# Input-projection weight tiles split by a casting load, a negated copy and an accumulating load

## The chip, the cores and the metric

The kernel runs on 1 core of one Trainium2 chip. The metric is device time of one execution in microseconds. Engines: TensorE (PE), VectorE (DVE), ScalarE (ACT), GpSimd (POOL) and SyncE (SP). SP and POOL issue DMAs, which run on the core's 16 DMA engines; the profile shows SP's transfers on the hardware queue q1 and POOL's on the software queue q0.

## What is computed

One inference step of a decoder layer (width 1024) for 512 prompt tokens and 8 sample tokens, 520 columns together. One input projection `w_in` of 8 x 1024 columns feeds a chunkwise recurrence (HGRN2, 8 heads of 128), a second recurrence (RG-LRU, 8 blocks of 128) and two merge gates; then come branch projections, an output projection and an MLP.

```python
h = _rmsnorm(x, norm1_g[l]) * (1.0 + sc1) + sh1
u = h @ w_in[l].astype(F32)
qa, fa, ia, oga, xb, yb, ga, gb = _split_cols(u)
...
merged = (jax.nn.sigmoid(ga) * (o_a @ w_branch_a[l].astype(F32))
          + jax.nn.sigmoid(gb) * (o_b @ w_branch_b[l].astype(F32)))
x = (x.astype(F32) + g1 * (merged @ w_out[l].astype(F32))).astype(dt)
h2 = _rmsnorm(x, norm2_g[l]) * (1.0 + sc2) + sh2
ff = jnp.square(jax.nn.relu(h2 @ w_ff1[l].astype(F32))) @ w_ff2[l].astype(F32)
x = (x.astype(F32) + g2 * ff).astype(dt)
```

## The kernel before

To keep float32 accuracy, the kernel splits each operand into a high part in the type float32r and the remainder, a low part in the same type, and adds three products: high by high, high by low, low by high (`products`, L148). The activations `h` are split once; the weights come in tiles of 1024 x 128 (in SBUF 128 x 8 x 128, 512 KB), and each tile is split when it arrives. A tile is used by `gemm` (L160): 8 steps of k, 3 products, 2 halves of the 520 columns, that is 48 matmuls of 260 columns into one PSUM pair `mm` (two such pairs rotate), 32 of them with the high part and 16 with the low one.

`weights` lists the tiles of the whole program up to the MLP in the order of use. The input projection has 56 whole tiles here: the first three are split by hand in `begin`, 53 pass through `ready_w` (L134), called by `take_w` as each tile is taken. It starts loads up to `LOADS` = 3 ahead of the split, and splits each tile `AHEAD` = 2 tiles before its use. A load (`_load_w`, L103) is issued by SP into `wst`, a pool of `WST` = 4 staging buffers of 512 KB. A split (`_split_w`, L107) is a cast on ScalarE to `whi` (L113) and a subtraction on VectorE to `wlo` (L116), both in the pool `whl`, with two pairs of buffers at this stage (`split_place` takes them in turn). Half of the last gate's columns are not whole tiles: they are loaded by POOL as `gw` (L866) and split in forms of their own.

The code is written as a list of steps (heads, recurrences, gates and so on); a scheduler decides the order of the instructions on each engine, which are then executed in that order. In `begin` the order on PE, ACT and DVE is the written one. POOL has little to do in the stage of the input projection: in the start the samples' columns (`fs`, `fsh`), and one root a head (`ss`, L231 and L232), which lies between ACT's sums of squares and ACT's scaling of that head's output. Later, in the MLP, POOL issues accumulating DMAs from SBUF to SBUF (`ma<-snap`, L1317 and L1335).

In the DMA issues, `wm<-in_w_piece` and `xT` are the first pieces that the program loads; the modulation of the input and the first products wait for them.

Of the kernel before, what the change touches and what calls it, by code (L numbers as in the profile page):

```python
# [6 lines left out]
F32 = mybir.dt.float32  # L7
F32R = mybir.dt.float32r
I32 = mybir.dt.int32
U8 = mybir.dt.uint8  # L10
AF = mybir.ActivationFunctionType
OP = mybir.AluOpType
# [8 lines left out]
KO = D // 128  # L21
# [9 lines left out]
NWM = 8  # L31
WST = 4
LOADS = 3
MODK = 7
FIRSTS = 3
ROWS = "rows"
MARK = "mark"
# [42 lines left out]
class Kernel:  # L80
# [7 lines left out]
    def weights(self, specs):  # L88


        self.wspecs, order, n = specs, [], 0
        for i, key in enumerate(specs):
            order.append((n - 1, 0, i) if ROWS in key else (n - AHEAD, 1, i))
            n += ROWS not in key
        self.worder = [(t, i) for t, _, i in sorted(order)]
        self.wstage, self.wsplit = {}, {}
        self.wnext_load = self.wnext_split = self.wcur = self.wtile = 0
        self.sw, self.nsplit, self.places = None, 0, []

    def _load_w(self, key, pool):  # L100
        src, r0, c0 = key[:3]
        st = pool.tile([128, KO, 128], F32, name="wst")
        self.nc.sync.dma_start(st.rearrange("p k n -> p (k n)"),  # L103
                               self.i[src][c0 // D - 2, r0 // 128] if ROWS in key else self.i[src][c0 // 128])
        return st

    def _split_w(self, st, place, after=None):  # L107
        if place is None:
            hi, lo = (self.wst.tile([128, KO, 128], F32R, tag="wst", name=n) for n in ("whi", "wlo"))
        else:  # L110
            pool = self.sw if place % 2 else self.whl
            hi, lo = (pool.tile([128, KO, 128], F32R, tag=f"{n}{place}", name=n, bufs=1) for n in ("whi", "wlo"))
        ins = self.nc.scalar.copy(hi, st)  # L113
        if after or self.start_act:
            self.behind(ins, after or self.start_act)
        self.nc.vector.tensor_tensor(lo, st, hi.bitcast(F32), OP.subtract)  # L116
        return hi, lo
# [15 lines left out]

    def ready_w(self, tile, loads=LOADS):  # L134
        while self.wnext_split < len(self.worder) and self.worder[self.wnext_split][0] <= tile:
            while self.wnext_load < min(self.wnext_split + loads, len(self.worder)):
                i = self.worder[self.wnext_load][1]
                self.wstage[i] = None if MARK in self.wspecs[i] else self._load_w(self.wspecs[i], self.wst)
                self.wnext_load += 1
            i = self.worder[self.wnext_split][1]  # L140
            st = self.wstage.pop(i)
            if ROWS in self.wspecs[i]:
                self.wsplit[i] = st.rearrange("p k n -> p (k n)")
            else:
                self.wsplit[i] = None if st is None else self._split_w(st, self.split_place())
            self.wnext_split += 1
# [13 lines left out]
    def gemm(self, keys, acts, extra=0, ps=None, after=None):  # L160

        ps = ps or self.pmm.tile([128, 2, 512], F32, name="mm")
        for q, key in enumerate(keys):
            hi, lo = self.take_w(key)
            for k in range(KO):
                n = q * KO + k
                self.products(ps, (hi[:, k], lo[:, k]), acts[n], n == 0, n == len(keys) * KO - 1, extra,
                              after=after)
                if self.mod_open and k == MODK:
                    self.mod_cols(*self.mod_open, after=self.last_product)  # L170
# [1904 lines left out]
```

## Time and profile before

| | |
|---|---|
| median of 3 runs (range) | 1007.01 us (1004.93 to 1007.44) |
| profiled execution | 1007.33 us, span 1005.5 us |
| busy PE, DVE, ACT, POOL | 985.9, 689.7, 524.4, 136.7 us |
| DMA hardware queue q1 | 123.47 MB, 36.3% of 16 engines |
| DMA software queue q0 | 18.70 MB, 8.5% of 16 engines |
| loads of `w_in` tiles (SP) | 56 of 512 KB, 3.6 us to landing |

Busy time of an engine is the time in which it executes at least one instruction. Matmuls are pipelined, so a group's mean duration is longer than the distance from one to the next. "Idle before" names what ended an engine's wait ahead of a group; the DMA rows give packets, MB and the share of 16 engines' time in the stretch that is asked for.

### The profile page before, as it was taken

The page shows a single profiled execution, that of the slowest core. Times are in us where ns is not written, and L with a number is a line of the kernel's source. Part 1 is how long each engine was busy: PE and PEld are TensorE (multiplying, and loading weights), DVE is VectorE, ACT ScalarE, POOL GpSimd, SP SyncE. Part 2 cuts the span into 40 slices and gives each one's busy share as a digit, 9 for nine tenths or more (in the row PEclk, how much of TensorE's full clock was granted, in tenths as well). Part 3 has the DMA queues.
Part 4 walks back from the last instruction along what each step waited for, and adds up shares of the span by engine and source line. Part 5 has one row for each costly group of instructions (what it writes and reads, how often), then busy time and mean ns, then how long its engine had stood idle before and what let it go on. Part 6 is the DMA issues. An engine that isn't in the chain of part 4 may idle for free. (4 is left out here: it accounts for less than half of the span.)

```text
span 1005.5 us, 23181 instructions
## 1 busy us (share of the span) xinstructions
PE 985.9 (98%) x9636; PEld 956.4 (95%) x9636; DVE 689.7 (69%) x1357; ACT 524.4 (52%) x997; POOL 136.7 (14%) x247
## 2 busy tenths in 40 slices
PE   7999999999999999989999999999999999999997
PEld 6899999999989999989999999999999999999996
DVE  6795966676595667886535456767767776768685
ACT  5565645734653572474412233466456645646662
POOL 1310000000000101121000000022321331232050
PEclk8999999999999999999999999999999999999999
DMA  9563343244234236345547665222752472272142
GB/s 348 216 209 128 102 159 124 81 145 132 98 133 153 100 99 212 111 148 179 185 168 270 241 212 199 84 85 53 177 151 81 104 192 85 65 183 70 64 85 86
DMA packets 48857, 143.67 MB, mean 143 GB/s; under 512 B 6240, under 2 KB 15904, under 8 KB 47720
## 3 DMA queue, kind: packets, MB, share of 16 engines
q1 hardware_dynamic: 37280, 123.47, 36.3%
q0 software_dynamic: 11456, 18.70, 8.5%
q8 instruction: 75, 1.23, 0.5%
q14 instruction: 30, 0.25, 0.1%
q10 hardware_dynamic: 16, 0.03, 0.0%
HBM read 123.65 MB, written 11.26 MB: 134 GB/s over the span
## 5 line engine op out<-in xcount | busy, mean ns | idle before, releaser
L155 PE MATMUL mm<-h,whi 128*128 128x260 f32 (+1 forms) x2720 | 451.6, 285 | 0.0
L155 PEld LDWEIGHTS mm<-h,whi 128*128 128x128 f32 x2720 | 378.5, 189 | 1.3 <-issue 0.6
L155 PE MATMUL mm<-h,wlo 128*128 128x260 f32 x1360 | 280.3, 286 | 2.6 <-DVE wlo L116 2.6
L116 DVE TENSOR_TENSOR wlo<-wst,whi 128x1024 fp32r<-128x1024 f32 x156 | 190.6, 1223 | 123.7 <-ACT whi L113 119.4
L113 ACT CAST whi<-wst 128x1024 fp32r<-128x1024 f32 x156 | 163.5, 1050 | 187.9 <-PE mm L155 147.3
L155 PEld LDWEIGHTS mm<-h,wlo 128*128 128x128 f32 x1360 | 212.4, 189 | 4.0 <-DVE wlo L116 3.2
L1293 POOL TENSOR_TENSOR ft<-ft,fsh 128x8 f32<-128x8 f32 x28 | 18.4, 658 | 209.1 <-DVE ft L1287 209.1
L1301 DVE TENSOR_TENSOR f<-f 128x260 f32<-128x260 f32 x64 | 27.3, 427 | 27.8 <-ACT f L1296 27.1
L1290 ACT ACTIVATE ft<-ft,fsh 128x512 f32<-128x512 f32 (+2 forms) x36 | 24.1, 676 | 36.1 <-DVE ft L1287 36.1
L155 PE MATMUL mm<-b,whi 128*128 128x260 f32 x256 | 41.6, 284 | 0.0
L155 PE MATMUL mm<-oa,whi 128*128 128x260 f32 x256 | 41.6, 285 | 0.0
L155 PE MATMUL mm<-a,whi 128*128 128x260 f32 x256 | 41.4, 284 | 0.0
L582 DVE TENSOR_TENSOR X<-X,tb 128x512 f32<-128x512 f32 x48 | 31.0, 688 | 12.6 <-PE ps L574 9.3
L155 PEld LDWEIGHTS mm<-oa,whi 128*128 128x128 f32 x256 | 34.9, 188 | 2.1 <-ACT whi L113 1.6
L155 PEld LDWEIGHTS mm<-b,whi 128*128 128x128 f32 x256 | 35.1, 189 | 1.7 <-ACT whi L113 1.2
L155 PEld LDWEIGHTS mm<-a,whi 128*128 128x128 f32 x256 | 35.0, 188 | 1.2 <-PE pt L359 0.8
L231 POOL TENSOR_SCALAR ss<-ss 128x4 f32<-128x4 f32 x8 | 2.7, 332 | 238.2 <-ACT g L666 238.1
L1335 POOL DMA_DIRECT2D ma<-snap x28 | 27.3, 989 | 37.5 <-issue 27.5
L179 ACT ACTIVATE gate<-pb,pa 128x260 f32<-128x260 f32 x32 | 15.4, 482 | 31.2 <-PE pb L714 31.2
L1317 POOL DMA_DIRECT2D ma<-snap x28 | 25.9, 926 | 41.0 <-DMA ma<-snap 25.6
L1296 ACT ACTIVATE f<-ft 128x520 f32<-128x520 f32 (+1 forms) x36 | 20.8, 587 | 15.0 <-POOL ft L1294 13.0
L155 PE MATMUL mm<-a,wlo 128*128 128x260 f32 x128 | 25.8, 283 | 0.0
(565 smaller groups left out, 2075.2 us busy)
## 6 DMA issues: line engine op xcount, KB each, us to landing
wst<-in_w_ff_dram SPq DMA_DIRECT2D x64, 512.0 KB, 3.7
wst<-in_w_in_dram SPq DMA_DIRECT2D x56, 512.0 KB, 3.6
wst<-in_w_mod_dram SPq DMA_DIRECT2D x32, 512.0 KB, 4.8
wm<-in_w_piece_dram SPq DMA_DIRECT2D x4, 1024.0 KB
wm<-in_w_rows_dram SPq DMA_DIRECT2D x4, 1024.0 KB, 11.4
st<-in_state_hgrn_dram SPq DMA_DIRECT2D x8, 512.0 KB, 3.9
vb<-vd SPq DMA_DIRECT2D x8, 512.0 KB, 3.9
out_dram<-st SPq DMA_DIRECT2D x8, 512.0 KB
```

The lines of the kernel that those rows point to most:

```text
L113: ins = self.nc.scalar.copy(hi, st)
L116: self.nc.vector.tensor_tensor(lo, st, hi.bitcast(F32), OP.subtract)
L155: self.last_product = self.nc.tensor.matmul(ps[s][:, :c.stop - c.start], x, y[:, c], start=first and n == 0, stop=last and n == 2)
L179: ins = self.nc.scalar.activation(out, x, AF.Sigmoid, **kw)
L231: p.tensor_scalar(out, x, n * EPS, None, OP.add)
L582: last = nc.vector.tensor_tensor(half, half, factors(tbs, x, b), OP.mult)
L1290: nc.scalar.activation(t[:, :p], t[:, :p], AF.Relu, bias=sh[:, 0:1])
L1293: eng.tensor_tensor(t[:, p:], t[:, p:], sh[:, 1:9], OP.add)
L1296: nc.scalar.activation(f, self.two(self.ft)[:, a:a + n], AF.Square)
L1301: self.nc.vector.tensor_tensor(f[:, n], f[:, a], f[:, b], op)
L1317: nc.gpsimd.dma_start(x[1][:, b], v[:, :n], accum_op=OP.add)
L1335: nc.gpsimd.dma_start(x[t][:, a], s[p], accum_op=OP.add)
```

## The change

The 53 tiles of `w_in` that pass through `ready_w` are split in another way. POOL issues a load that casts the tile from HBM into the float32r buffer of the high part (`_cast_w`, L117 in the changed file); ScalarE writes the negated high part into the low part's buffer (`_rest_w`, L122); POOL issues a second load of the same tile from HBM that adds it to that buffer (L125). Odd tiles take a pair of `whl`, even ones two of the four `wst` buffers, so four tiles have buffers at once. The cast of the next tile is issued in the code before the rest of the present one (`CASTS` = 2). All other tiles keep the former way.

```diff
+CASTS = 2
...
+    def _cast_w(self, key):
+        src = self.i[key[0]][key[2] // 128]
+        self.ncast += 1
+        if self.ncast % 2:
+            place = self.split_place()
+            hi, lo = (self.whl.tile([128, KO, 128], F32R, tag=f"{n}{place}", name=n, bufs=1) for n in ("whi", "wlo"))
+        else:
+            hi, lo = (self.wst.tile([128, KO, 128], F32, name="wst").bitcast(F32R) for _ in range(2))
+        self.nc.gpsimd.dma_start(hi.rearrange("p k n -> p (k n)"), src)
+        return hi, lo, src
+
+    def _rest_w(self, hi, lo, src):
+        ins = self.nc.scalar.activation(lo, hi.bitcast(F32), AF.Copy, scale=-1.0)
+        if self.start_act:
+            self.behind(ins, self.start_act)
+        self.nc.gpsimd.dma_start(lo.rearrange("p k n -> p (k n)"), src, accum_op=OP.add)
+        return hi, lo
...
     def ready_w(self, tile, loads=LOADS):
         while self.wnext_split < len(self.worder) and self.worder[self.wnext_split][0] <= tile:
-            while self.wnext_load < min(self.wnext_split + loads, len(self.worder)):
+            cast = self.wspecs[self.worder[self.wnext_split][1]][0] == "w_in"
+            while self.wnext_load < min(self.wnext_split + (CASTS if cast else loads), len(self.worder)):
                 i = self.worder[self.wnext_load][1]
-                self.wstage[i] = None if MARK in self.wspecs[i] else self._load_w(self.wspecs[i], self.wst)
+                key = self.wspecs[i]
+                self.wstage[i] = None if MARK in key else self._cast_w(key) if key[0] == "w_in" else self._load_w(key, self.wst)
...
-            if ROWS in self.wspecs[i]:
+            if self.wspecs[i][0] == "w_in":
+                self.wsplit[i] = self._rest_w(*st)
+            elif ROWS in self.wspecs[i]:
```

The scheduler places the new instructions. In the listings a row is a line of the code, the instruction, and what it writes from what; the names are the program's tiles with a buffer number.

POOL at the program's start, first before and then after the change:

```order
L237 IOTA jp_160 128x128
L247 MEMSET halfc_170 128x1
L72 TENSOR_TENSOR fs_123<-xsr_122,modT_108 128x16
L72 CAST h_157<-fs_123 128x2x8
L72 TENSOR_TENSOR h_158<-fs_123,h_157 128x2x8
```

```order
L262 IOTA jp_160 128x128
L272 MEMSET halfc_170 128x1
L117 DMA whi_471<-in_w_in_dram 128x1024
L117 DMA whi_670<-in_w_in_dram 128x1024
L117 DMA wst_474<-in_w_in_dram 128x1024
L73 TENSOR_TENSOR fs_123<-xsr_122,modT_108 128x16
L73 CAST h_157<-fs_123 128x2x8
```

Three casting loads now stand ahead of the samples' columns, near the start of the program.

POOL in the middle of the input projection, around the first two roots, first before and then after; L117 is the casting load, L125 the accumulating one:

```order
L256 IOTA hs_780 128x128
L231 TENSOR_SCALAR ss_1593<-ss_1593 128x4
L232 TENSOR_TENSOR ss_1593<-ss_1593,halfc_170 128x4
L231 TENSOR_SCALAR ss_1638<-ss_1638 128x4
L232 TENSOR_TENSOR ss_1638<-ss_1638,halfc_170 128x4
```

```order
L117 DMA whi_2044<-in_w_in_dram 128x1024
L125 DMA wlo_2045<-in_w_in_dram 128x1024
L256 TENSOR_SCALAR ss_1583<-ss_1583 128x4
L257 TENSOR_TENSOR ss_1583<-ss_1583,halfc_170 128x4
L117 DMA wst_2143<-in_w_in_dram 128x1024
L125 DMA wst_2144<-in_w_in_dram 128x1024
L117 DMA whi_2238<-in_w_in_dram 128x1024
L125 DMA wlo_2239<-in_w_in_dram 128x1024
L117 DMA wst_2297<-in_w_in_dram 128x1024
L125 DMA wst_2298<-in_w_in_dram 128x1024
```

Where POOL had nothing between the roots, the two loads of one tile now follow each other, then those of the next tile; the accumulating load stands ahead of the next tile's cast.

ACT in the same place after the change (before it, the cast `whi<-wst` stood where L122 stands); L122 is the negated copy, and `mm_2043` is the PSUM pair of the tile three before `whi_2044`:

```order
L122 ACTIVATE wlo_2045<-whi_2044 128x1024
L691 ACTIVATE g_1582,ss_1583<-pt_1574 128x128
L691 ACTIVATE g_1582,ss_1583<-pt_1574 128x128 x3
L750 COPY xb_2097<-mm_2043 128x520
L696 ACTIVATE g_1582<-pt_1574,ss_1583 128x128
L696 ACTIVATE g_1582<-pt_1574,ss_1583 128x128 x3
L122 ACTIVATE wst_2144<-wst_2143 128x1024
L234 CAST xcs_2109<-xc_2099 128x520
L750 COPY xb_2196<-mm_2142 128x520
```

The eviction of a tile's PSUM pair stands behind the negated copy of the tile three later and ahead of the one after that.

More of the change, by code (lines that the diff above doesn't have):

```diff
@@ L97, in weights @@
         self.wnext_load = self.wnext_split = self.wcur = self.wtile = 0
-        self.sw, self.nsplit, self.places = None, 0, []
+        self.sw, self.nsplit, self.ncast, self.places = None, 0, 0, []
     def _load_w(self, key, pool):
```

## The prediction

> **What bounds the kernel now.** I began with the page's first part, then cut the program into stages, listed that stage's groups and waits, and last read the DMA views for what an issue, a load and an accumulating load cost.
>
> ```profile
> span 1005.5 us, 23181 instructions
> PE 985.9 (98%) x9636; PEld 956.4 (95%) x9636; DVE 689.7 (69%) x1357; ACT 524.4 (52%) x997; POOL 136.7 (14%) x247
> ...
> 0.00:47.00 47.00, 41.57 (x374) 33.12 (x375) 31.66 (x88) 24.78 (x44) 8.67 (x27) 0.93 0.74 287
> 47.00:435.00 388.00, 384.54 (x4546) 376.53 (x4546) 277.09 (x624) 211.61 (x436) 25.56 (x43) 1.00 0.40 131
> ```
>
> In the rows by stage the columns are the stretch, its length, busy time and count of PE, weight load, DVE, ACT and POOL, the granted clock, the DMA engines' busy share and GB/s. TensorE is at work 98% of the span. The stage that the change touches, the products of the input projection after the first three tiles, is 47 to 435: PE idles 3.46 us of 388 there, at full clock. The profiled execution took 1007.33 us; its span is 1.8 less, and the median of the runs, 1007.01, stands 0.3 below it. I count from 1007.3.
>
> ```profile
> L155 PE MATMUL mm<-h,whi 128*128 128x260 f32 x1696 | 284.3, 285 | 0.0
> L155 PE MATMUL mm<-h,wlo 128*128 128x260 f32 x848 | 175.5, 286 | 2.6 <-DVE wlo L116 2.6
> L116 DVE TENSOR_TENSOR wlo<-wst,whi 128x1024 fp32r<-128x1024 f32 x52 | 63.6, 1224 | 68.2 <-ACT whi L113 65.1 <-PE ps L565 3.1
> L113 ACT CAST whi<-wst 128x1024 fp32r<-128x1024 f32 x52 | 54.5, 1048 | 65.1 <-PE mm L155 56.3 <-issue 8.0 <-ACT at L602 0.9
> ```
>
> These are the groups of that stage. A tile has 32 products with its high part, so 1696 are 53 tiles: one every 388 / 53 = 7.3 us. The split costs ACT 1.05 and DVE 1.22 us a tile and waits mostly for PE to give a buffer back (56.3 us): it is early. PE waited 2.6 us in all for the low parts.
>
> **What the change removes.** 53 subtractions on DVE, 53 x 1.22 = 65 us, all beside PE but for the 2.6 us of PE's wait. ACT keeps one operation of the same 128x1024 shape a tile (a negated copy for the cast): nothing either way. SP loses 53 issues. No product changes. So the most that can be won is the 3.46 us of PE's idling.
>
> **What it adds.** A tile now takes two software DMAs on POOL's queue, and the second needs ACT, which needs the first. The trace has software loads of the same 512 KB (gw) and accumulating DMAs from SBUF (ma<-snap), but no casting and no accumulating load from HBM.
>
> ```profile
> L866 POOL DMA_DIRECT2D gw<-in_w_gate_dram x8: 527/544/552, 388.1 to 459.2; - x8
> DMA to landing us min/median/max: 3.7/6.8/10.3
> ...
> L1335 POOL DMA_DIRECT2D ma<-snap x28: 847/862/2159, 698.6 to 966.8; - x28
> ...
> q0 software_dynamic: 144, 0.52, 27.7%
> gw<-in_w_gate_dram POOLq DMA_DIRECT2D x1, 512.0 KB, 4.3
> ...
> q0 software_dynamic: 288, 0.26, 30.6%
> ma<-snap POOLq DMA_DIRECT2D x2, 126.0 KB, 3.8
> ma<-snap POOLq DMA_DIRECT2D x1, 130.0 KB, 2.8
> ...
> q0 software_dynamic: 576, 2.10, 50.4%
> gw<-in_w_gate_dram POOLq DMA_DIRECT2D x4, 512.0 KB, 8.7
> ```
>
> The first three rows are from the views by tile (duration of an issue in ns, min, median and max; landing counted from issue). The other pairs are the DMA view cut to 453 to 459, 698 to 704 and 388 to 400 us: packets, MB, share of the 16 engines. One gw load alone keeps the engines 27.7% of 6 us = 1.66 us and lands after 4.3, so 2.6 us of it are fixed. Two accumulating DMAs, 0.26 MB, take 30.6% of 6 us = 1.84 us, or 3.7 us for the 0.52 MB of a tile: over twice a plain load. Four gw loads queued behind each other land after 8.7 in the median: on one queue a DMA waits for the data ahead of it.
>
> Now the order of POOL's queue decides. From about the eighth tile it is cast of tile t, accumulating load of t, cast of t+1, one by one, though four tiles have buffers: the accumulating load stands in front of the next cast and waits for ACT. One round, counted from one accumulating issue:
> - its data ends after 2.6 (fixed) + 3.7 = 6.3 us; the cast, issued 0.86 later, has its data behind it, 1.66 more: it lands at about 8.0.
> - the negated copy 1.05, two hand-overs 0.2, and ACT's queue ahead of it: ACT is busy 211.61 of 388, mostly with operations of about 0.6 us, so 0.2 to 0.5.
> - SP's other transfers (states, broadcasts, outputs) cross it on the same 16 engines; they now take 40% of them with the w_in loads, about 22% without: 0.2 us more.
>
> That makes 9.8 us a tile against the 7.3 that PE needs. POOL's queue would set the pace and PE would stand 2.5 us a tile. Bounds: if the cast need not wait for the accumulating data ahead of it, 0.86 + 4.3 + 1.05 + 0.5 = 6.7 us, below 7.3, all hidden (the row of one gw). If the cast itself costs what an accumulating DMA does (3.7 for 1.66), 11.8 us. I take the plain price, since a cast reads one stream like gw, where the accumulating DMA reads two.
>
> Then the sum. About 44 tiles pay: 44 x (9.8 - 7.3) = 110. The first ones don't, since three casts leave at the program's start and the next go two and two; the buffers give the chain a lead of about one round, -10. POOL's own small work stands in the same chain now:
>
> ```profile
> L232 POOL TENSOR_TENSOR ss<-ss,halfc 128x4 f32<-128x4 f32 x8 | 9.7, 1218 | 0.7
> L231 POOL TENSOR_SCALAR ss<-ss 128x4 f32<-128x4 f32 x8 | 2.7, 332 | 238.2 <-ACT g L666 238.1
> ```
>
> Six of these eight roots lie between two of the new DMAs, 6 x 1.55 = +9; what they wait for on ACT is three tiles older, so no wait is added. The other way round, ACT's evictions stand behind negated copies that wait for casts; PE's next bank then comes about when the next accumulating load is issued, which shifts PE by a few us once and does not change the round.
>
> The start:
>
> ```profile
> DMA  0267999999999999999999999998970004800006
> GB/s 0 48 75 259 403 363 396 415 464 423 380 401 402 388 397 419 423 430 430 396 403 389 440 427 430 423 375 246 410 307 14 0 0 89 335 14 0 0 14 140
> q1 hardware_dynamic: 3785, 13.58, 74.0%
> ...
> 12.30 2.28 PE L72 MATMUL mm<-h,fhi 128*128 128x260 f32 x8 [2.19 <-ACT h L72]
> 45.32 1.52 PE L72 MATMUL pb<-wst,shp 128*32 128x128 f32 x48
> ```
>
> This is the DMA view of the first 48 us (slices of 1.2 us), PE's first product, and its last reading of the raw first tiles. The engines are full from 4 to 33 us at about 0.41 MB a us. Three casts (1.57 MB) now come from POOL's queue beside the first pieces that PE's chain waits for: up to 1.57 / 0.41 = 3.8 us later, after which PE is continuous. Bounds 0 and 4; I take 4, since nothing holds those casts back. So +110 - 10 + 9 + 4 = +113: 1120 us.
>
> **Two rules beside the rows.** The Trainium skill (DMA: Bandwidth & Descriptors, Anatomy of one DMA — SWDGE (gpsimd) path) fits a software DMA as about 2.0 us plus bytes / 436e3. For 512 KB that estimates 3.2 us where the gw row has 4.3; with it and no queueing a round is 5.6 us and everything hides, as in the first rival below. The Trainium skill (SBUF — State Buffer, Who interferes with whom) also has DVE's two-port modes starve the descriptor writing of software DMAs, which would lengthen the issues. The gw issues here stay within 527 to 552 ns; only single ma<-snap issues reach 2.2 us; so I add nothing for it.
>
> **Rivals.**
> - The chain hides. If DMAs overlap on the queue, a round is 6.7 us and only the start and the second tile are left (its low part needs a staging buffer that PE reads until 46.8 us): 4 + 3, 1014 us. For it speaks the 4.3 of a lone gw; against it the 8.7 of four queued ones. It decides below a round of 7.3.
> - The cast costs as much as the accumulation: 44 x 4.5 + 3 = +201, 1208 us. No row shows a casting DMA.
> - Faster. DVE's relief takes away PE's waits: at most 3.46 us, 1004 us. It needs a round under 7.3 and first casts that do not delay the start's pieces, while these rows show the engines full there.
> - The removed work is no relief at all, being beside PE, and the added DMAs too are beside it: no change, 1007. It is the first rival with a start that costs nothing.
>
> **How the numbers follow.** I give 0.62 to the queue's round at plain cast price, 0.17 to the dear cast, 0.13 to the hidden chain, 0.04 to no change and 0.04 to faster. The likeliest gives 1120; by itself it runs from 1058 (a round of 8.4, the cast's data half overlapped) to 1195 (11.5, the cast nearly at the dear price). To leave out no more than 2 in 10 the range goes down to the hidden chain, 1012, and up to 1215. 0.3% (3 us) is about what a measurement here can tell from no change; faster 0.04, within 0.05 (a little of the hidden chain with it), slower 0.91.
>
> **What would show it.** Right: PE's share in 47 to 435 and beyond falls to about 75%, its waits in the products with the low part name software DMAs; POOL's accumulating issues stand some 9.8 us apart and wait for ACT's negated copy, which waits for the cast; software DMAs land after 6 to 8 us; DVE's busy time is 65 us less and nothing comes of it. Wrong: accumulating issues 7.3 us apart with PE full (hidden), or casts that land after 4 us right behind an accumulating load; a software queue whose time per MB is the same for casts as for accumulations (dear cast); a first product much later than 16 us.

## The result, and the profile after

| | before | after |
|---|---|---|
| median (range), 4 runs each | 1007.1 us (1004.93 to 1007.44) | 1077.74 us (1075.56 to 1081.69) |
| span of the profiled execution | 1005.5 us | 1073.7 us |
| first product of the start, first one of a whole tile (L155, L180) | 12.30, 46.8 us | 15.34, 50.4 us |
| first product of the last gate | 434.8 us | 507.4 us |

The changed kernel takes 1.071 times as long (95% interval 1.0693 to 1.0727). The landmarks in the last rows say where: the start is 3.6 us later, the stretch from the first whole tile to the last gate grows from 388.0 to 457.0 us (+69.0), and what follows gives some 4 us back.

These lines of the page and of the table by stage answer to the first fence of the prediction; the second stage now ends at 505.

```profile
span 1073.7 us, 23262 instructions
PE 1002.7 (93%) x9636; PEld 968.5 (90%) x9636; DVE 635.3 (59%) x1304; ACT 525.3 (49%) x997; POOL 212.2 (20%) x353
...
0.00:47.00 47.00, 38.89 (x310) 30.42 (x311) 29.00 (x83) 22.24 (x40) 9.56 (x25) 0.85 0.86 312
47.00:505.00 458.00, 402.31 (x4588) 389.82 (x4588) 225.81 (x578) 215.09 (x441) 100.52 (x151) 0.96 0.67 168
```

PE idles 458 - 402.3 = 55.7 us in that stage instead of 3.5. Its busy time grew too, from 384.5 to 402.3 us for nearly the same products, and the granted clock in the same row is 0.96 instead of 1.00. So the 69 us are 52 of standing and some 17 of slower products (the last section shows what slowed them).

The view of waits up to 520 us: who waited for whom, the total, how often, the longest.

```profile
POOL wlo L125 <- ACT wlo L122: 141.7, 23, 9.6
POOL wst L125 <- ACT wst L122: 138.2, 24, 9.3
...
ACT wst L122 <- DMA wst<-in_w_in_dram: 93.0, 22, 7.8
ACT wlo L122 <- DMA whi<-in_w_in_dram: 82.0, 19, 7.5
...
PE pb L739 <- ACT gate L204: 16.4, 10, 3.6
PE pt L670 <- ACT g L665: 7.2, 3, 4.2
PE ps L595 <- DVE X L607: 6.7, 4, 5.1
PE mm L180 <- DMA wst<-in_w_in_dram: 5.6, 1, 5.6
```

POOL's accumulating loads (L125) wait for the negated copies (L122), and these for the casts: the loop that the prediction drew. But only one of PE's waits names a transfer, that of the second tile. The others name ACT for 37.6 us and DVE for 12.3: ACT's evictions and gates stand in its queue behind a negated copy that waits for its cast. One such case, two lines of ACT's timeline and one of PE's (start, duration, and in brackets the idle time before and what ended it):

```profile
186.55 1.06 ACT L122 ACTIVATE wlo<-whi 128x1024 fp32r<-128x1024 f32 x1 [6.30 <-DMA whi<-in_w_in_dram]
187.51 0.46 ACT L204 ACTIVATE gate<-pb,pa 128x260 f32<-128x260 f32 x1
...
188.03 0.51 PE L739 MATMUL pb<-xcs,bdh 128*128 128x260 f32 x2 [1.75 <-ACT gate L204]
```

PE needs the bank `pb`, which the gate on ACT has to empty first.

One round of the loop, POOL's timeline first, then ACT's.

```profile
143.71 0.85 POOL L125 DMA_DIRECT2D wst<-in_w_in_dram  x1 [8.76 <-ACT wst L122]
144.27 0.86 POOL L117 DMA_DIRECT2D whi<-in_w_in_dram  x1
152.45 0.85 POOL L125 DMA_DIRECT2D wlo<-in_w_in_dram  x1 [7.32 <-ACT wlo L122]
...
151.09 1.06 ACT L122 ACTIVATE wlo<-whi 128x1024 fp32r<-128x1024 f32 x1 [6.57 <-DMA whi<-in_w_in_dram]
```

The cast leaves 0.56 us after the accumulating load, ACT can read it 6.8 later, and 1.4 after that the next accumulating load leaves: 8.74 us. From 88.32 to 483.4 us there are 45 such rounds, 8.78 us in the mean with the roots in them. The views by tile have both loads (landing from issue in us, min, median, max; first the casts, L117, then the accumulating loads, L125):

```profile
DMA to landing us min/median/max: 3.9/6.6/9.3
...
DMA to landing us min/median/max: 5.3/5.6/9.5
```

### The profile page after: what moved, and what is told of

Its sections match the earlier page's. It is cut to its first block, busy times and chain, and to the rows that moved or that the text cites. A ratio compares the mean times of both kernels' runs of the same rounds, so it can differ in the third digit from the quotient of the medians.

```text
span 1073.7 us, 23262 instructions
## 1 busy us (share of the span) xinstructions
PE 1002.7 (93%) x9636; PEld 968.5 (90%) x9636; DVE 635.3 (59%) x1304; ACT 525.3 (49%) x997; POOL 212.2 (20%) x353
## 5 line engine op out<-in xcount | busy, mean ns | idle before, releaser
L180 PE MATMUL mm<-h,whi 128*128 128x260 f32 x1888 | 315.8, 287 | 0.0
L180 PEld LDWEIGHTS mm<-h,whi 128*128 128x128 f32 x1888 | 266.1, 191 | 0.8 <-issue 0.2
L180 PE MATMUL mm<-h,wlo 128*128 128x260 f32 (+1 forms) x944 | 195.8, 287 | 0.0
L180 PE MATMUL mm<-h,wst 128*128 128x260 f32 x1248 | 171.1, 290 | 5.6 <-DMA wst<-in_w_in_dram 5.6
L134 ACT CAST whi<-wst 128x1024 fp32r<-128x1024 f32 x104 | 109.2, 1053 | 121.4 <-PE mm L180 87.1
L180 PEld LDWEIGHTS mm<-h,wst 128*128 128x128 f32 x1248 | 160.1, 194 | 6.8 <-ACT ma L1952 5.8
L137 DVE TENSOR_TENSOR wlo<-wst,whi 128x1024 fp32r<-128x1024 f32 x104 | 127.0, 1223 | 55.3 <-ACT whi L134 54.1
L180 PEld LDWEIGHTS mm<-h,wlo 128*128 128x128 f32 x944 | 149.5, 191 | 0.2
L122 ACT ACTIVATE wst<-wst 128x1024 fp32r<-128x1024 f32 x26 | 27.5, 1059 | 102.2 <-DMA wst<-in_w_in_dram 93.0
L122 ACT ACTIVATE wlo<-whi 128x1024 fp32r<-128x1024 f32 x26 | 27.6, 1060 | 94.2 <-DMA whi<-in_w_in_dram 82.0
L125 POOL DMA_DIRECT2D wlo<-in_w_in_dram x27 | 23.9, 887 | 153.2 <-ACT wlo L122 141.7
L125 POOL DMA_DIRECT2D wst<-in_w_in_dram x26 | 22.7, 873 | 148.2 <-ACT wst L122 138.2
L180 PE MATMUL mm<-b,whi 128*128 128x260 f32 x256 | 41.6, 284 | 0.0
L180 PE MATMUL mm<-oa,whi 128*128 128x260 f32 x256 | 41.6, 284 | 0.0
L180 PE MATMUL mm<-a,whi 128*128 128x260 f32 x256 | 41.4, 284 | 0.0
L180 PEld LDWEIGHTS mm<-oa,whi 128*128 128x128 f32 x256 | 34.8, 188 | 2.1 <-ACT whi L134 1.6
L180 PEld LDWEIGHTS mm<-b,whi 128*128 128x128 f32 x256 | 35.1, 188 | 1.7 <-ACT whi L134 1.2
L180 PEld LDWEIGHTS mm<-a,whi 128*128 128x128 f32 x256 | 35.0, 188 | 1.2 <-issue 0.8
```

The costliest lines, as they stand in the source:

```text
L122: ins = self.nc.scalar.activation(lo, hi.bitcast(F32), AF.Copy, scale=-1.0)
L125: self.nc.gpsimd.dma_start(lo.rearrange("p k n -> p (k n)"), src, accum_op=OP.add)
L180: self.last_product = self.nc.tensor.matmul(ps[s][:, :c.stop - c.start], x, y[:, c], start=first and n == 0, stop=last and n == 2)
```

## The experiments

**1. The other order on POOL.** The accumulating load of a tile stands behind the cast of the next one; nothing else is changed.

```diff
-        self.nc.gpsimd.dma_start(hi.rearrange("p k n -> p (k n)"), src)
+        self.last_cast = self.nc.gpsimd.dma_start(hi.rearrange("p k n -> p (k n)"), src)
...
-        self.nc.gpsimd.dma_start(lo..., src, accum_op=OP.add)
+        self.behind(self.nc.gpsimd.dma_start(lo..., src, accum_op=OP.add), self.last_cast)
```

> One constraint more on POOL's queue: the accumulating load of tile t is issued behind the cast of tile t+1. Theory Q (the queue's round: the accumulating load waits for ACT, and the next cast waits behind it): each cast now leaves a round earlier, the waits of POOL's accumulating issues for the negated copy (280 us in the changed kernel) nearly vanish, tiles follow in 7.3 us, and only the start's 3.0 us and the 5.6 us at the second tile stay: 1012 to 1022 us. Theory B (the DMA engines: 28 MB more and 328 ns for an accumulating packet of 4 KB): same traffic, 1065 to 1085. Theory L (four pairs of buffers are too few for casting, negating and accumulating): the earlier cast only waits for PE instead, 1065 or more.

Measured: 1015.96 us, ratio 1.0088 (1.0056 to 1.012). The stage from 47 to 435, and POOL's timeline in it:

```profile
47.00:435.00 388.00, 377.29 (x4516) 369.60 (x4516) 218.43 (x558) 214.91 (x435) 99.91 (x149) 1.00 0.81 196
...
139.43 0.56 POOL L117 DMA_DIRECT2D wst<-in_w_in_dram  x1 [7.41 <-PE mm L180]
139.98 0.90 POOL L125 DMA_DIRECT2D wlo<-in_w_in_dram  x1
145.63 0.56 POOL L117 DMA_DIRECT2D whi<-in_w_in_dram  x1 [4.76 <-PE mm L180]
147.49 0.86 POOL L125 DMA_DIRECT2D wst<-in_w_in_dram  x1 [1.30 <-ACT wst L122]
```

All the loads and copies are still there, with the DMA engines busy 81% of the time instead of 67%, and 62 of the 71 us are gone. POOL now waits for PE to give buffers back, that is, it is early. The order of two DMAs in one queue was nearly all of the loss.

**2. The same order, without the wait.** The negated copy reads the high part of the tile before (so a low part holds its tile minus the high part of another); POOL's order stays that of the changed kernel.

```diff
-        ins = self.nc.scalar.activation(lo, hi.bitcast(F32), AF.Copy, scale=-1.0)
+        ins = self.nc.scalar.activation(lo, (self.prev_hi or [hi])[0].bitcast(F32), AF.Copy, scale=-1.0)
...
+        self.prev_hi = [hi]
```

> The negated copy reads the high part of the tile before, so that it does not wait for this tile's cast (the low parts are wrong); every instruction and transfer stays. Theory Q: the round loses its ring cast, copy, accumulating load; 1012 to 1022 us. Theory B: 1065 to 1085. Theory A (ACT: evictions stand behind copies that wait for casts, and PE waits for these): also near 1015, since the copies wait no more.

Measured: 1013.86 us, ratio 1.0074 (1.0046 to 1.0101). With the same bytes, issues and order, the loss goes when the copy need not wait for the cast just issued. Bandwidth is out.

**3. The negation on POOL.**

```diff
-        ins = self.nc.scalar.activation(lo, hi.bitcast(F32), AF.Copy, scale=-1.0)
+        self.nc.gpsimd.tensor_scalar(lo, hi.bitcast(F32), -1.0, None, OP.mult)
```

> The negated copy is made by POOL instead of ACT, so nothing on ACT stands behind a copy that waits for a cast. Theory Q: the round stays and its copy is no shorter on POOL (1 to 2 us against 1.06): 1070 to 1120 us, with PE waiting for the low parts' DMAs instead of ACT. Theory A: PE's waits for ACT (gate, g, X) go and nothing takes their place: 1010 to 1035.

Measured: 1044.03 us, ratio 1.0362 (1.0331 to 1.0393), between the two expectations. It tells less than it was meant to, since the scheduler changed the order with it:

```profile
L122 POOL TENSOR_SCALAR wlo<-whi x27: 2761/2773/3034, 5.5 to 454.1; 128x1024 fp32r<-128x1024 f32 x27
...
121.34 0.60 POOL L117 DMA_DIRECT2D wst<-in_w_in_dram  x1
121.94 0.93 POOL L123 DMA_DIRECT2D wlo<-in_w_in_dram  x1
125.70 0.56 POOL L117 DMA_DIRECT2D whi<-in_w_in_dram  x1 [2.82 <-PE mm L178]
```

The next cast stands ahead of many of the accumulating loads (L123 here), as in the first experiment; in its place POOL pays 2.77 us a copy where ACT paid 1.06. PE's waits in its stage (47 to 475 us) still tell something: they name ACT for 4.6 us and transfers for 11.0, where the changed kernel has 37.6 and 5.6. So PE meets a late cast through ACT's evictions while the copies are ACT's, and through late transfers when they are not. How the whole loss divides between the two stays open.

**4. Half of the accumulation.** Only four of the eight blocks of the low part are added, 256 KB (the rest of the low part stays the negated high part).

```diff
-        self.nc.gpsimd.dma_start(lo.rearrange("p k n -> p (k n)"), src, accum_op=OP.add)
+        self.nc.gpsimd.dma_start(lo[:, :KO // 2].rearrange("p k n -> p (k n)"), src[:, :D // 2], accum_op=OP.add)
```

> The accumulating load adds only the first half of each row (256 KB instead of 512; the other half of the low part stays the negated high part). Theory Q with the cast's data queued behind the accumulating data: 8 packets of 328 ns an engine, 2.6 us, become 1.3; the cast lands 1.3 us earlier, a round is 7.5 instead of 8.8: 1015 to 1035 us. If the round is made of fixed latencies and the data ahead is hidden: 1065 to 1080.

Measured: 1047.42 us, ratio 1.0396 (1.031 to 1.0481): a gain, but less than expected. The two runs are 14 us apart, and the views are of the slower one. Casts, then accumulating loads:

```profile
DMA to landing us min/median/max: 3.7/5.9/10.1
...
DMA to landing us min/median/max: 3.8/4.1/6.8
```

The accumulation lands 1.5 us sooner, the cast behind it only 0.7. The DMA packets of the traces tell why (medians of over 30 rounds). In the changed kernel the cast's first packet starts 4.2 us after its issue, just where the accumulating load's last packets run out. Here it starts after 2.7 us, again where they run out: 1.5 us sooner, as expected. But from there to the end of the cast's last packet it takes 2.9 us instead of 2.1. So the cast does wait for the data ahead of it, and half of what was won is lost behind; why its own packets take longer stays open.

**5. Casting loads without accumulation.** VectorE subtracts again, from a tile that SP loads beside the cast; two pairs of buffers, as before the change.

```diff
-            hi, lo = (self.wst.tile([128, KO, 128], F32, name="wst").bitcast(F32R) for _ in range(2))
...
-        return hi, lo, src
+        return hi, lo, self._load_w(key, self.wst)
...
+        self.nc.vector.tensor_tensor(lo, src, hi.bitcast(F32), OP.subtract)
```

> The casting load stays, the accumulating load and the negated copy go: VectorE subtracts again, from a tile that SP loads beside the cast; two pairs of buffers as in the kernel before. Theory Q (a casting load costs what a plain one does; the loss lies in the accumulating load that stands in front of the next cast): nothing waits for an accumulation, a tile's chain is cast 4.1 + subtraction 1.2 + hand-overs 0.2 = 5.5 us behind the release of its buffer, below PE's 7.3; left are the casts in the start (+3): 1008 to 1016 us. Rival C (the cast itself is dear, like an accumulation): 7 us and more a chain, many of 50 tiles late by 1 us or more: 1040 us or more.

Measured: 1033.59 us, ratio 1.0288 (1.0271 to 1.0305): neither. The cast is cheap, and still the kernel loses 28 us.

```profile
POOL whi L113 <- PE mm L173: 258.9, 40, 14.1
...
DVE wlo L118 <- DMA whi<-in_w_in_dram: 37.9, 18, 5.4
...
DMA to landing us min/median/max: 3.6/4.6/8.4
```

A cast can leave only when PE gives its high part's buffer back (L113 waits 40 times for that), then DVE's queue waits for it 18 times (37.9 us) with other work behind it. The 5.5 us of the expectation left no room for those queues. This is read from the waits; no run tested it by itself. Experiment 9 asks what casts cost with four tiles in flight.

**6. Two tiles in flight.** As the changed kernel, every tile in the two pairs of `whl`.

```diff
-        if self.ncast % 2:
+        if True:
```

> As the changed kernel, but every tile uses the two pairs of buffers of the high and low parts, so two tiles are in flight instead of four. If buffers matter: tile t+2 can only be cast when PE ends tile t, and is ready 4.1 + 1.05 + 5.6 + 0.3 = 11 us later; a pair of tiles then takes 11 + 7.3 us, 9.15 a tile, 50 x 1.85 = +92 and the start +4: about 1100 us (1085 to 1130). If the queue's order alone sets the round, 8.8 us as in the changed kernel: 1070 to 1085.

Measured: 1162.48 us, ratio 1.1559 (1.1514 to 1.1605). Buffers matter, and more than expected; its stage, and PE's largest wait (up to 520 us):

```profile
47.00:590.00 543.00, 440.52 (x4596) 422.20 (x4595) 232.57 (x586) 226.15 (x448) 102.31 (x156) 0.89 0.59 146
...
PE mm L180 <- DMA wlo<-in_w_in_dram: 66.7, 25, 5.9
```

Here the low parts do come late at PE itself. The clock is 0.89, at which PE's 7.3 us a tile become 8.2; the expectation's (11 + 7.3) / 2 = 9.15 a tile then is (11 + 8.2) / 2 = 9.6, and 50 x (9.6 - 7.3) + 4 = 119 of the 155 us. The accumulating issues stand 10.2 us apart in the mean (50 rounds from 70 to 580 us), which gives 149. What makes a pair of tiles 1.2 us longer than that sum stays open.

**7. The first casts held back.** They stand on POOL behind the first operation on the samples' columns.

```diff
-            pool.tensor_tensor(fs[:, k], xsr[:, k], ..., OP.mult)
+            ins = pool.tensor_tensor(fs[:, k], xsr[:, k], ..., OP.mult)
+            self.first_fs = self.first_fs or ins
...
-        self.nc.gpsimd.dma_start(hi.rearrange("p k n -> p (k n)"), src)
+        self.behind(self.nc.gpsimd.dma_start(hi.rearrange("p k n -> p (k n)"), src), self.first_fs)
```

> As the changed kernel, but the three casts of the start stand on POOL behind the first operation on the samples' columns, which runs at about 12.5 us, when the first pieces are in. If those casts delay the start: PE's first product comes back to about 12.3 us and the program gains 3 to 3.6 us: 1073 to 1075. If the start is late for another reason, or the 3 us are given back later in the queue's round: 1076 to 1079.

Measured: 1078.74 us, ratio 1.0731 (1.0711 to 1.0751), no gain. PE's first product did come early, at 11.77 us, but then:

```profile
23.50 0.24 POOL L1947 TENSOR_SCALAR ong<-pa 128x1 f32<-128x1 f32 x1 [2.53 <-DMA pa<-in_params_dram]
...
24.55 1.46 PE L73 MATMUL mm<-h,fhi 128*128 128x260 f32 x7 [2.67 <-POOL h L73]
51.62 0.51 PE L180 MATMUL mm<-h,whi 128*128 128x260 f32 x2
```

The casts at 10 us now met the parameters instead of the first pieces; POOL waited for them ahead of the next samples' columns, PE for POOL, and the first whole tile came at 51.6 instead of 50.35. The delay had moved to the next transfer.

**8. Three repairs.** The order of the first experiment, the hold of the seventh, and `if self.ncast % 4 in (1, 2)` in the place of `% 2`, so that tiles 1 and 2 take `whl`.

> Three repairs together: the accumulating load of a tile stands behind the cast of the next one (as in the first experiment, 1015.96), the first casts stand behind the first operation on the samples' columns, and tiles 1 and 2 both take the pairs of the high and low parts (tiles 3 and 4 the staging buffers, and so on), so that tile 2 needs no staging buffer that PE still reads. If the 5.2 us of waiting for tile 2 and the 3.0 us of the start are what is left of the first experiment's loss: 1006 to 1010, no change from the kernel before. If the casts and accumulations cost PE something beside that (clock, contention): 1011 to 1015. Faster than 1004 would need PE's remaining waits to go as well; nothing seen says so.

Measured: 1013.26 us, ratio 1.0079 (1.0065 to 1.0092), no better than the first. The start stands as in the seventh, and tile 2 is late for a reason other than its buffer; ACT's timeline shows it (L73 is the start, L123 the negated copies):

```profile
53.02 2.56 ACT L73 ACTIVATE h<-xT,shp 128x512 fp32r<-128x512 f32 x4
55.49 1.04 ACT L123 ACTIVATE wlo<-whi 128x1024 fp32r<-128x1024 f32 x1
...
PE mm L181 <- DMA wlo<-in_w_in_dram: 4.4, 1, 4.4
```

The copy of tile 2 is kept behind the shift of the activations (`start_act`). Before the change a subtraction of 1.2 us followed there, now an accumulating load of over 5 us.

**9. No accumulation.** The changed kernel without its accumulating loads (the low parts hold only the negated high parts).

```diff
-        self.nc.gpsimd.dma_start(lo.rearrange("p k n -> p (k n)"), src, accum_op=OP.add)
```

> The changed kernel with the casting loads, the negated copies and four tiles in flight, but without the accumulating loads: the low part holds only the negated high part. Theory Q (the loss comes from the accumulating load that stands in front of the next cast): casts run ahead, every copy is early, and only the start's 3 us are left: 1008 to 1014 us, POOL's waits on ACT's L122 gone. Rival C (casting loads and copies alone, as in the fifth experiment with 1033.6, cost 20 us or more): 1025 us or more.

Measured: 1004.03 us, ratio 0.9983 (0.9974 to 0.9992), faster than either expectation. Casts (they land after 3.8 us in the median) and copies cost nothing when they may run ahead. With the start still as late as in the changed kernel (50.3), it says that something is also won.

The DMA views (packets, MB, share of the 16 engines) of a cast here, 111 to 117 us, and of an accumulating load in the changed kernel, 152 to 157 us, where POOL's queue moves 122 of that load's 144 packets and nothing else:

```profile
q0 software_dynamic: 144, 0.52, 28.4%
...
q0 software_dynamic: 122, 0.50, 59.4%
```

The cast keeps the engines for 28.4% of 6 us = 1.7 us, as the plain `gw` did, the accumulating load for 59.4% of 5 us = 3.0 us, with other transfers crossing it.

**10. The start mended.** Experiment 8 with the casts behind the third operation on the samples' columns, and tile 2's copy behind tile 1's.

```diff
-            self.first_fs = self.first_fs or ins
+            self.first_fs = ins if i < 3 else self.first_fs
...
-        if self.start_act:
+        if self.nsplit < 3 and self.first_rest:
+            self.behind(ins, self.first_rest)
+        elif self.start_act:
             self.behind(ins, self.start_act)
+        self.first_rest = self.first_rest or ins
```

> The eighth experiment (1013.26) with two edits in the start: the first three casts stand behind the third operation on the samples' columns (about 27 us) instead of the first (10 us), so that they meet no piece and no parameter that PE's chain waits for; and the negated copy of tile 2 stands behind that of tile 1 on ScalarE instead of behind the shift of the activations (55.5 us). If what was left is the start: the first whole tile comes back from 52.3 to about 47 us, the 4.4 us of waiting for tile 2 go, and the time is 1004 to 1008, no change from the kernel before. If the two software loads a tile cost PE something in the middle of the projection as well: 1009 to 1012.

Measured: 1002.31 us against 1006.02 (10 and 21 runs), ratio 0.9967 (0.9956 to 0.9978). It is 0.33% faster than the kernel before, and below the expected range: the first whole tile is at 48.1 us, tile 2 waits for nothing.

```profile
span 1000.2 us, 23244 instructions
PE 982.5 (98%) x9636; PEld 954.7 (95%) x9636; DVE 632.5 (63%) x1304; ACT 527.7 (53%) x997; POOL 213.2 (21%) x353
...
47.00:435.00 388.00, 384.17 (x4584) 376.92 (x4577) 225.49 (x579) 216.83 (x441) 101.54 (x151) 1.00 0.81 200
435.00:510.00 75.00, 75.00 (x664) 70.69 (x664) 48.37 (x84) 37.44 (x70) 6.92 (x13) 1.00 0.52 180
```

The projection is as full as before the change (384.17 of 388 against 384.54); what is won lies behind it. The same stretch before the change, PE's waits in it, and the products that mark it (in the view by line: ns, then the first and last start):

```profile
435.00:510.00 75.00, 71.74 (x611) 67.51 (x610) 49.39 (x89) 38.33 (x73) 9.64 (x18) 0.98 0.51 177
...
PE mm L910 <- DVE wgate L884: 1.2, 1, 1.2
PE mm L910 <- ACT gp L921: 1.0, 1, 1.0
PE mm L910 <- ACT wgate L883: 1.0, 1, 1.0
...
L910 PE MATMUL mm<-h,wgate x96: 278/283/364, 434.8 to 486.1; 128*128 128x260 f32 x96
L155 PE MATMUL mm<-b,wlo x128: 277/283/288, 486.4 to 536.6; 128*128 128x260 f32 x128
```

From the first product of the last gate to the last one with `b` it is 101.8 us before, 97.8 in the changed kernel (507.4 to 605.2) and 96.3 in the tenth. In the fifth, where VectorE subtracts as before the change, it is 97.4, so the 4 us are not VectorE's relief in the projection. They are PE's waits for the split of the last gate's weights (`wgate`) and for an eviction (`gp`), 3.2 us, and a spell of 3.4 us at half clock behind the last two of them (454.4 to 457.8 us, PE busy throughout), worth 1.7. The changed kernel has one such wait of 0.9 us, the tenth none, and neither has the spell. Which of the scheduler's moves took them away was not tried.

## Why the prediction was right, and its loss too large, step by step

The forecast was 1120 us, a loss of 113; the measured loss is 70.6. Direction and mechanism were right, the size was 60% too large. That the time lies in the range says little by itself: 1012 to 1215 also holds the hidden chain and the dear cast, and the experiments decide between them.

- **PE's bound and POOL's loop: right.** Order (1), dependence (2) and the accumulating load itself (9) each remove nearly all of the loss by themselves. The rival of the hidden chain, 1014 us, is what the kernel does when the order lets it: 1015.96 and 1013.86.
- **The round: 9.8 forecast, 8.78 measured.** The mis-sized term is the accumulating load, 6.3 us to its end; from HBM it lands after 5.6, so 3.0 us over the fixed 2.6 instead of 3.7. The DMA view agrees (3.0, ninth experiment). The rows of `ma<-snap`, much smaller transfers inside SBUF, were the wrong scale. That is 0.7 of the 1.0; the rest is in the allowances for queues and crossing traffic (0.6 to 0.9). The one for SP's other transfers took them at 22% of the engines, and the changed kernel's stage has 12.3% on SP's queue. 45 x (8.78 - 7.3) = 67 against 69.0 measured, where the sum had 44 x 2.5 - 10 + 9 = 109: the round is the whole overshoot. The roots' +9 lie inside the measured rounds, and the lead of -10 was not seen apart from them.
- **"On one queue a DMA waits for the data ahead of it": right.** The cast lands after 3.8 us with no accumulation ahead (9) and 6.6 behind a whole one. Its first packet starts 1.2 us after its issue in the ninth and 4.2 in the changed kernel, where the accumulating load's packets have run out (fourth experiment).
- **Casts at the plain price: right.** 1.7 us of the engines, like the lone gw, and 3.8 us to landing in the median of the ninth against its 4.3. The Trainium skill (DMA: Bandwidth & Descriptors, Anatomy of one DMA — SWDGE (gpsimd) path) gives an estimate of 3.2; no cast here landed before 3.6. The dear cast, 1208 us, is out.
- **The start, +4: right in size** (first whole tile +3.6). But the range's lower end, 0, needed more than a later place: casts at 1.4 us delayed pieces, at 10 us parameters, and only at 28 us nothing that PE needed soon.
- **PE's waits: wrong.** They were to name software DMAs in the low parts' products; apart from tile 2 they name ACT and DVE. The step that failed is that ACT's evictions shift PE "by a few us once": POOL's round is indeed unchanged by them, but with four tiles in flight the low parts are early, and it is through those evictions that PE meets the delay of round after round. With two tiles (6) the low parts are late, as forecast. About 75% of PE's time was forecast, 88% was measured, because the round was shorter and the products themselves got slower.
- **The removed work: its size right, its worth not.** All 53 subtractions are gone. DVE's busy time fell by 54 us and not by 65, because neighbours on DVE overlap (the durations added up fall by 63), and the projection won nothing. That at most 3.46 us could be won looked at one stage only: PE stood another 3.3 us in the last gate. That the ninth and the tenth come close to the faster rival's 1004 is luck, since its reason, DVE's relief in the projection, is not theirs.

## What to carry to other kernels

A queue that executes in order turns two independent chains into one: when an issue that waits for a compute engine stands ahead of the next tile's first load, buffers for four tiles do not hide the wait, and putting the load first costs nothing. Price each new round trip by its landing time against the pace of the bound engine, and then look at the first tiles by themselves, where a longer chain meets orders that were written for the shorter one. When a start is full of transfers, moving an added one only chooses what it delays, until it stands behind the last that is urgent.

## What was not expected of the hardware

An interrupted TensorE also ran slower. In the stage of the projection of seven kernels, PE's busy share and the granted clock: 99% and 1.00 before, 97% and 1.00 in the first experiment, 95% and 0.97 in the fifth, 94% and 0.98 in the third, 91% and 0.97 in the fourth, 88% and 0.96 after the change, 81% and 0.89 in the sixth (stretches of 388 to 543 us from 47 on; the two ends and the changed kernel are in the fences above). PE's busy time for much the same products rises with it: 384.5, 402.3, 440.5 us.

The traces show how. Their clock records hold two values, 1.00 and 0.50. Three rows of 3.4 us from the changed kernel (columns as in the first fence of the prediction): PE stands, then works at half clock, then at full clock again.

```profile
104.00:107.40 3.40, 0.00 (x0) 0.00 (x0) 0.00 (x0) 1.30 (x2) 0.00 (x0) 1.00 0.22 77
107.40:110.80 3.40, 3.22 (x15) 3.15 (x16) 0.28 (x1) 1.10 (x4) 1.42 (x2) 0.50 0.55 75
110.80:114.20 3.40, 3.35 (x83) 3.05 (x82) 0.43 (x2) 0.57 (x1) 0.00 (x0) 1.00 0.83 235
```

In the changed kernel's stage there are seven such spells of 3.4 or 6.8 us, 34 us together. PE is busy for 26.2 of these with work that takes half as long at full clock, so some 13 of the 17 us are theirs; the other 4 were not traced. Each spell begins in a wait of PE of 2.1 to 5.6 us or within 1 us of its end; two waits of 2.5 and 2.6 us have none behind them. (In the last gate before the change one follows two waits of 1.0 and 1.2 us close together.) In the sixth there are 25 spells, 116 us together, in this stage of the kernel before none. So a stall costs more than its length, here some 17 us on 52. The waits come first and the half clock after them; that the idling lowers the clock was not tested by a run of its own.
